# Tiles that TensorE reads in a hybrid decoder layer, placed at multiples of 128 bytes

## Chip, cores and metric

The kernel runs on one core of one Trainium2 chip. The time is the device time of one launch in microseconds, the median of several runs. The profile is one execution of the same program, with every engine's instructions.

## The reference, cut to what matters

One decoder layer over 256 tokens of width 2048, batch 1, float32: a mixer of sliding-window attention beside a Mamba-2 state space part, then a causal convolution FFN.

```python
def _hybrid_mixer(xn, w_in, ...):
    proj = xn @ w_in                       # 2048 -> 9248 columns: q, k, v, z, xbc, dt
    ...
    attn = _rmsnorm(_sliding_window_attention(q, k, v, sinks), attn_out_norm)
    xbc = jax.nn.silu(_causal_dwconv(xbc, ssd_conv_w, ssd_conv_b))
    ...
    y = _ssd_chunked(xs, dt, a, bm, cm) + ssd_d[:, None] * xs
    y = _gated_group_rmsnorm(y, z, ssd_norm)
    return jnp.concatenate([attn, y], axis=-1) @ w_out      # 4096 -> 2048

def _conv_ffn(hn, w_up, ffn_conv_w, ffn_conv_b, w_down):
    u = _causal_dwconv(hn @ w_up, ffn_conv_w, ffn_conv_b)   # 2048 -> 11264
    gate, val = u[..., :D_FF], u[..., D_FF:]
    return (jax.nn.silu(gate) * val) @ w_down               # 5632 -> 2048

h = x
h = h + _hybrid_mixer(_rmsnorm(h, norm_mix), ...)
h = h + _conv_ffn(_rmsnorm(h, norm_ffn), ...)
return _rmsnorm(h, norm_final)
```

The weights are 2048 x 9248, 4096 x 2048, 2048 x 11264 and 5632 x 2048 numbers, float32. Each is read once.

## The kernel before

All large products run in the type float32r, which TensorE takes at one column a cycle. To keep float32 accuracy each operand is split in two parts, hi and lo, with hi + lo equal to the number, and a product is three matmuls: hi x hi, hi x lo and lo x hi.

The weights come in blocks of 1 MB through SyncE's queue into raw (three buffers of 8704 bytes a partition). `split` makes hi on ScalarE (L70) and lo on VectorE (L72; a fourth of them on GpSimd while the mixers run) into four buffers each, 4352 bytes a partition. The activations lie transposed, channels on partitions, with both parts side by side: xT (the normed input), later h2T in the same place, attT (attention's output) and yT (the state space part's output), each 128 partitions x 16 channel tiles x 2 parts x 256 tokens.

The large products come in two forms. `gemm_tok` holds the activations stationary and moves 512 columns of weights (L156 to L158): keys with dt first (cut into 256 and 288 columns), values, four of queries and four of z from xT, then eight of the output projection from attT and yT. The down projection (`w_down_part`, `down`) has the same three lines with gs, the two parts of the gated activations of one channel tile, as the stationary operand. `gemm_chan` holds the weights stationary and moves activations: in the state space part three matmuls of 256 columns (L217 to L219, `wide=False`); in the up projection one of 512 columns, both parts of h2T at once under hi (L225), and one of 256 columns under lo (L223).

In a row such as `L156 PE MATMUL acc<-hi,xT` the first name behind the arrow is the moving operand, the second the stationary one.

The order is: keys and values (to about 80 us), four query products with attention beside them (to about 280 us), the state space part with three products a turn (to about 525 us), output projection (to 705 us), up projection with its convolutions (to 1190 us), down projection and the final norm. Work beside the large products is put between their turns by `later` and `step`; a scheduler of the tile framework then sets each engine's order. Tiles are placed by pools: a pool lays its tiles one behind the other in the order in which they are first asked for, each at a multiple of 32 bytes unless the tile asks for another multiple.

`steps_dt` works out the time steps of the state space part (softplus by a series) on VectorE, with four tiles sp0 to sp3 of 256 bytes a partition; `rope`, which rotates keys and queries, has two tiles rpa and rpb of 512 bytes.

Of the kernel before, what the change touches and what calls it, by code (L numbers as in the profile page):

```python
# [10 lines left out]
F32 = mybir.dt.float32  # L11
F32R = mybir.dt.float32r
# [35 lines left out]
def hymba(ctx, tc, x, xt, w_kd, w_in, w_out, w_up, w_down, par, vecs, gfin, con, out):  # L48
# [16 lines left out]
    share = [0, 0]  # L65

    def split(raw, o, n):
        hi = wp.tile([P, RAWW // 2], F32R, tag="hi", name="hi", bufs=4)
        lo = wp.tile([P, RAWW // 2], F32R, tag="lo", name="lo", bufs=4)
        A.copy(out=hi[:, :n], in_=raw[:, o : o + n])  # L70
        share[1] += 1
        (G if share[0] and share[1] % share[0] == 0 else V).tensor_tensor(  # L72
            out=lo[:, :n], in0=raw[:, o : o + n], in1=hi[:, :n].bitcast(F32), op=ALU.subtract
        )
        return hi, lo

    def pieces(src, width, parts, load=None, work=None):
        """the parts of a block's splits; load, work: what goes before a part's load and split."""
        raw = wp.tile([P, RAWW], F32, tag="raw", name="raw", bufs=3)
# [14 lines left out]
    xT = cp.tile([P, NKT, 2, S], F32R, tag="xT", name="xT")  # L94
# [22 lines left out]
    def rstd(dst, ss, n):  # L117
        """dst = (ss / n + EPS) ** -0.5, a column for each of the token tiles."""
# [4 lines left out]
    def rows_of(dst, r):  # L123
        """dst[p, t] = r of token t, on every partition."""
# [7 lines left out]
    def split_T(dst, kt, src, g, view=lambda a: a):  # L132
        """dst[:, kt] = the two parts of src * g."""
# [6 lines left out]
    def transpose_split(src, ct0, dst, kt0, n, gbase):  # L140
        """src [tokens, t, channels] to the parts of its transpose, n channel tiles times their weights."""
# [18 lines left out]
    # work beside the large products: steps that come up so many turns after they are called for  # L160
# [13 lines left out]
    def gemm_tok(blocks, actT, evac, width=2048, cuts=((0, 512),), tag="acc", parts_of=None):  # L174
        """out[token, column]: activations stationary, weights moving."""
# [24 lines left out]
    def gemm_chan(blocks, actT, evac, tag="acc", wide=True):  # L200
        """out[channel, token]: weights stationary, activations moving; wide: in two sums for evac to add."""
# [29 lines left out]
    def conv(dst, b, rB, wcol, bias, taps, wide):  # L231
        """dst = causal convolution over tokens of b * rB, channels on partitions."""
        u = up.tile([P, S], F32, tag="cu", name="cu", bufs=3)
# [14 lines left out]
    attT = mixctx.enter_context(tc.tile_pool(name="mp0", bufs=1)).tile([P, NKT, 2, S], F32R, name="attT")  # L248

    # =========== attention ===========  # L250
# [10 lines left out]
    def norm_x():  # L261
# [3 lines left out]
        for h in range(2):  # L265
            xq = wp.tile([P, RAWW], F32, tag="raw", name="x_r", bufs=3)[:, :D].rearrange("p (t d) -> p t d", t=NT)
# [11 lines left out]
    def rope(tl, t, nh):  # L278
        """rotate the first ROT dims of each head of tl[:, t] (nh heads), in place."""
# [26 lines left out]
    x_of = lambda kt: (xT, kt)  # noqa: E731  # L306
# [33 lines left out]
    # time steps: dt = softplus(dtx), cumulated dt * a  # L340
    nd = NT * NH
    f2 = lambda a: a.rearrange("p t h -> p (t h)")  # noqa: E731
# [6 lines left out]
    def steps_dt():  # L349
        ta, tb, tcc, td = (ap.tile([P, nd], F32, tag=f"sp{i}", name=f"sp{i}") for i in range(4))  # L350
# [50 lines left out]
    share[0] = 4  # part of the splits on GpSimd, beside what VectorE does for the mixers  # L401
# [5 lines left out]
    # values of two heads in two parts, with zeros on both sides: [v | 0] and [0 | v]  # L407
# [6 lines left out]
    def attention(c, q_t):  # L414
        """steps for two key-value heads 2 * c + jj and their query heads, q_t [P, t, (g, jj), HD]."""
        # on the partitions the two parts of a query beside each other, and for each of them the key's
# [34 lines left out]
        def scores(jj):  # L451
# [4 lines left out]
            for n in range(NT):  # L456
# [3 lines left out]
                for g0 in range(0, QPK, nh):  # L460
# [14 lines left out]
                    if n:  # L475
                        # the window: of each key's place in its block, either block's or none of it
# [27 lines left out]
        def probs_T(jj):  # L504
            """probabilities in two parts, keys on partitions; of the second block those of either block's keys."""
# [64 lines left out]
    # =========== state space ===========  # L570
# [419 lines left out]
```

## Time and profile before

| | us |
|---|---|
| median of 3 runs | 1442.59 |
| lowest and highest | 1442.48, 1445.29 |
| span of the profiled execution | 1442.0 |
| TensorE busy in it, 7925 matmuls | 1406.4 |
| VectorE busy | 989.6 |
| ScalarE busy | 772.0 |
| GpSimd busy | 269.4 |

The busy time of TensorE counts from a matmul's start to its modelled end, and consecutive matmuls overlap; how fast it goes is read from the distance between starts. PE in the rows is TensorE's matmuls, PEld its weight loads, DVE VectorE, ACT ScalarE, POOL GpSimd. The profile was taken on the one core that the kernel uses.

### The profile page before, as it was taken

How to read it: one execution, taken by the hardware profiler on the slowest of the kernel's cores; microseconds unless marked ns; L12 is line 12 of the kernel's file. 1: busy time of each engine (PE TensorE's matmuls, PEld its weight loads, DVE VectorE, ACT ScalarE, POOL GpSimd, SP SyncE). 2: the span in 40 equal slices, each digit the busy share in tenths (PEclk: the TensorE clock that was granted, in tenths of full speed). 3: DMA queues.
4: the chain of work that ended last, by engine and by line, in shares of the span. 5: the costliest groups of instructions: out<-in, count | busy, mean ns of one | idle time of the engine just before them, and what ended most of it. 6: DMA issues, size and time to landing. Idle time of an engine off the chain costs nothing.

```text
span 1442.0 us, 20476 instructions
## 1 busy us (share of the span) xinstructions
PE 1406.4 (98%) x7925; PEld 1231.3 (85%) x7925; DVE 989.6 (69%) x1454; ACT 772.0 (54%) x1209; POOL 269.4 (19%) x187
## 2 busy tenths in 40 slices
PE   8999999899999999999999999999999999999997
PEld 8888888789999988888888888888888888888886
DVE  6579999788685755555577776867767767545555
ACT  6565677456555554344465554555555554444444
POOL 0124544443434330000000111101111001000001
PEclk9999999999999999999999999999999999999999
DMA  8643333445545456554655555555555455555552
GB/s 317 237 166 125 117 118 117 140 153 190 182 172 186 155 175 257 179 201 175 226 180 195 187 181 200 187 193 190 190 187 192 176 204 190 190 204 182 197 199 94
DMA packets 40561, 263.37 MB, mean 183 GB/s; under 512 B 4608, under 2 KB 5248, under 8 KB 10640
## 3 DMA queue, kind: packets, MB, share of 16 engines
q1 hardware_dynamic: 38560, 254.69, 49.4%
q0 software_dynamic: 1904, 7.37, 1.8%
q8 instruction: 62, 1.02, 0.3%
q14 instruction: 35, 0.29, 0.1%
HBM read 259.92 MB, written 2.13 MB: 182 GB/s over the span
## 4 chain that ended last, share of the span: by engine, by line
PE 81%; DVE 10%; ACT 3%; issue 3%; POOL 1%; DMA 1%; SPq 0%; DVEq 0%; POOLq 0%; ACTq 0%
PE acc L225 11%; PE aux L225 11%; PE acc L158 10%; PE acc L157 10%; PE acc L156 10%; PE aux L223 6%; PE acc L223 6%; PE aux L156 3%; PE aux L157 3%; PE aux L158 3%; DVE lo L72 3%; DVE u L242 2%; PE acc L219 1%; PE acc L218 1%; PE acc L217 1%
## 5 line engine op out<-in xcount | busy, mean ns | idle before, releaser
L72 DVE TENSOR_TENSOR lo<-raw,hi 128x1024 fp32r<-128x1024 f32 (+2 forms) x442 | 550.0, 1250 | 348.9 <-ACT hi L70 348.3
L70 ACT CAST hi<-raw 128x1024 fp32r<-128x1024 f32 (+2 forms) x474 | 492.2, 1047 | 451.7 <-PE acc L158 135.3
L225 PE MATMUL acc<-h2T,hi 128*128 128x512 f32 x704 | 243.4, 391 | 0.0
L225 PE MATMUL aux<-h2T,hi 128*128 128x512 f32 x704 | 243.0, 391 | 0.0
L223 PE MATMUL aux<-h2T,lo 128*128 128x256 f32 x704 | 191.1, 282 | 0.0
L223 PE MATMUL acc<-h2T,lo 128*128 128x256 f32 x704 | 191.0, 282 | 0.0
L225 PEld LDWEIGHTS aux<-h2T,hi 128*128 128x128 f32 x704 | 129.8, 188 | 24.6
L225 PEld LDWEIGHTS acc<-h2T,hi 128*128 128x128 f32 x704 | 129.8, 188 | 24.5
L217 PE MATMUL acc<-xT,hi 128*128 128x256 f32 x512 | 145.4, 285 | 0.0
L218 PE MATMUL acc<-xT,hi 128*128 128x256 f32 x512 | 144.7, 283 | 0.0
L219 PE MATMUL acc<-xT,lo 128*128 128x256 f32 x512 | 143.9, 282 | 0.0
L817 POOL TENSOR_TENSOR gT<-gate,cv 128x256 f32<-128x256 f32 x44 | 61.2, 1392 | 434.5 <-DVE cv L242 424.0
L223 PEld LDWEIGHTS acc<-h2T,lo 128*128 128x128 f32 x704 | 132.9, 189 | 3.9
L223 PEld LDWEIGHTS aux<-h2T,lo 128*128 128x128 f32 x704 | 132.9, 189 | 3.8
L156 PE MATMUL acc<-hi,xT 128*128 128x512 f32 (+1 forms) x320 | 117.6, 387 | 6.4 <-ACT hi L70 5.7
L157 PE MATMUL acc<-lo,xT 128*128 128x512 f32 (+1 forms) x320 | 122.5, 386 | 0.6 <-DVE lo L72 0.6
L158 PE MATMUL acc<-hi,xT 128*128 128x512 f32 (+1 forms) x320 | 122.1, 384 | 0.0
L72 POOL TENSOR_TENSOR lo<-raw,hi 128x1024 fp32r<-128x1024 f32 x32 | 82.7, 2584 | 146.3 <-ACT hi L70 146.2
L218 PEld LDWEIGHTS acc<-xT,hi 128*128 128x128 f32 x512 | 97.1, 190 | 0.4
L217 PEld LDWEIGHTS acc<-xT,hi 128*128 128x128 f32 x512 | 97.0, 190 | 0.4
L219 PEld LDWEIGHTS acc<-xT,lo 128*128 128x128 f32 x512 | 96.9, 190 | 0.2
L156 PEld LDWEIGHTS acc<-hi,xT 128*128 128x128 f32 x320 | 60.4, 195 | 17.1 <-ACT hi L70 5.7
(224 smaller groups left out, 2421.9 us busy)
## 6 DMA issues: line engine op xcount, KB each, us to landing
raw<-in_w_up SPq DMA_DIRECT2D x88, 1024.0 KB, 4.8
raw<-in_w_in SPq DMA_DIRECT2D x68, 1024.0 KB, 4.8
raw<-in_w_down SPq DMA_DIRECT2D x44, 1024.0 KB, 4.8
raw<-in_w_out SPq DMA_DIRECT2D x32, 1024.0 KB, 4.8
e<-acs_d POOLq DMA_DIRECT2D x8, 512.0 KB, 6.2
raw<-in_w_kd SPq DMA_DIRECT2D x6, 544.0 KB, 7.8
x_r<-in_x SPq DMA_DIRECT2D x2, 1024.0 KB, 5.3
h<-in_x POOLq DMA_DIRECT2D x4, 512.0 KB, 7.5
```

The lines of the kernel that those rows point to most:

```text
L70: A.copy(out=hi[:, :n], in_=raw[:, o : o + n])
L72: (G if share[0] and share[1] % share[0] == 0 else V).tensor_tensor(out=lo[:, :n], in0=raw[:, o : o + n], in1=hi[:, :n].bitcast(F32), op=A ...
L156: PE.matmul(out=o, lhsT=lh, rhs=rh, start=first, stop=False)
L157: PE.matmul(out=o, lhsT=lh, rhs=rl, start=False, stop=False)
L158: PE.matmul(out=o, lhsT=ll, rhs=rh, start=False, stop=last)
L217: PE.matmul(out=b[ct][:, :S], lhsT=wh, rhs=rh, start=kt == 0, stop=False)
L218: PE.matmul(out=b[ct][:, :S], lhsT=wh, rhs=actT[:, kt, 1, :], start=False, stop=False)
L219: PE.matmul(out=b[ct][:, :S], lhsT=wl, rhs=rh, start=False, stop=end)
L223: PE.matmul(out=b[ct][:, :S], lhsT=wl, rhs=rh, start=False, stop=False)
L225: PE.matmul(out=b[ct], lhsT=wh, rhs=actT[:, kt, :, :], start=kt == 0, stop=end)
L242: V.scalar_tensor_tensor(out=dst[:, j:], in0=u[:, : S - j], scalar=wcol(taps - 1 - j), in1=dst[:, j:], op0=ALU.mult, op1=ALU.add,)
L817: G.tensor_tensor(out=gT[:, i, :], in0=gate[:, ct, :], in1=dst, op=ALU.mult)
```

## The change

Tiles that TensorE reads in the large products, and some that stand between them in a pool, are asked for with `align_bytes=128`: hi, lo, raw (and x_r in its place), xT, h2T, attT, yT, gs, gT, and the convolutions' u, gate and cu. So that the space suffices, two of the four tiles of `steps_dt` are no longer their own but rpa and rpb. Comments and docstrings are gone too.

```diff
 def split(raw, o, n):
-    hi = wp.tile([P, RAWW // 2], F32R, tag="hi", name="hi", bufs=4)
-    lo = wp.tile([P, RAWW // 2], F32R, tag="lo", name="lo", bufs=4)
+    hi = wp.tile([P, RAWW // 2], F32R, tag="hi", name="hi", align_bytes=128, bufs=4)
+    lo = wp.tile([P, RAWW // 2], F32R, tag="lo", name="lo", align_bytes=128, bufs=4)
...
-    raw = wp.tile([P, RAWW], F32, tag="raw", name="raw", bufs=3)
+    raw = wp.tile([P, RAWW], F32, tag="raw", name="raw", align_bytes=128, bufs=3)
...
-xT = cp.tile([P, NKT, 2, S], F32R, tag="xT", name="xT")
+xT = cp.tile([P, NKT, 2, S], F32R, tag="xT", name="xT", align_bytes=128)
...
-    u = up.tile([P, S], F32, tag="cu", name="cu", bufs=3)
+    u = up.tile([P, S], F32, tag="cu", name="cu", align_bytes=128, bufs=3)
...
-attT = mixctx.enter_context(tc.tile_pool(name="mp0", bufs=1)).tile([P, NKT, 2, S], F32R, name="attT")
+attT = mixctx.enter_context(tc.tile_pool(name="mp0", bufs=1)).tile([P, NKT, 2, S], F32R, name="attT", align_bytes=128)
...
 def steps_dt():
-    ta, tb, tcc, td = (ap.tile([P, nd], F32, tag=f"sp{i}", name=f"sp{i}") for i in range(4))
+    ta, tb, tcc, td = (ap.tile([P, nd], F32, tag=t, name=t, bufs=1) for t in ("sp0", "sp1", "rpa", "rpb"))
...
-    gs = fp.tile([P, 2, S], F32R, tag="gs", name="gs", bufs=4)
+    gs = fp.tile([P, 2, S], F32R, tag="gs", name="gs", align_bytes=128, bufs=4)
```

yT, h2T, gT, gate, x_r and the state space u change in the same way. Where the tiles stand in the two built programs, as the address of a partition's first byte modulo 128 and modulo 256 (all buffers of a name agree, and the slices that the large products read begin at multiples of 256 bytes within a tile, those of the key product at multiples of 128):

| tile | before, mod 128 | before, mod 256 | after, mod 128 | after, mod 256 |
|---|---|---|---|---|
| xT, h2T | 0 | 128 | 0 | 128 |
| hi, lo | 96 | 96 | 0 | 128 |
| attT, yT, gs | 96 | 96 | 0 | 0 |
| con_t (identity, masks) | 0 | 128 | 96 | 224 |
| qs, ks (query and key parts) | 32 | 160 | 64 | 64 |
| vs (value parts) | 32 | 160 | 64 | 64 |
| pt, po (probability parts) | 96 | 96 | 0 | 0 |

The order of instructions is the same on TensorE, ScalarE, GpSimd and SyncE. On VectorE it differs in one place, at about 47 us, where the time steps (L351 to L368) run between the rotations of the keys (L286 to L295) and the splits (L72); sp and rpa, rpb are the tiles named above:

```order
 L351 SCALAR_TENSOR_TENSOR sp_492<-dtx 128x64
-L364 TENSOR_SCALAR sp_495<-dtx 128x64
 L286 TENSOR_TENSOR rpa<-k_t,con_t 128x128
 L287 TENSOR_TENSOR rpb<-k_t,con_t 128x8x8
```

```order
 L355 TENSOR_SCALAR sp_493<-sp_492 128x64
+L364 TENSOR_SCALAR rpb<-dtx 128x64
 L356 RECIPROCAL sp_493<-sp_493 128x64
 L357 TENSOR_TENSOR sp_492<-sp_492,sp_493 128x64
 L358 TENSOR_TENSOR sp_493<-sp_492 128x64
-L359 TENSOR_SCALAR sp_494<-sp_493 128x64
-L360 TENSOR_TENSOR sp_494<-sp_494,sp_493 128x64
```

The maximum of dtx with zero (L364) stands before the second rotation's first rows in the kernel before and behind the first step of the series now; the rest of the series keeps its place under other names.

## Rows read from the trace of the kernel before

**Rows 1.** The page: span, and granted clock in 40 slices (9 is full).

```profile
span 1442.0 us, 20476 instructions
...
PEclk9999999999999999999999999999999999999999
```

**Rows 2.** The chain, shares by line, of 80-280, 340-525, 525-705, 705-1190, 1190-1430 us.

```profile
by line: issue 10.6%; DVE lo L72 9.9%; DVE u L242 8.4%; DVE pt L524 7.0%; PE acc L158 5.8%; PE acc L156 5.8%; PE acc L157 5.6%; ACT sm L486 4.4%; ACT hi L70 4.0%; DVE rs L496 3.7%; POOL sm L499 3.3%; DVE pt L515 3.1%; DVE sm L479 2.9%; DVE 
...
by line: PE acc L157 11.9%; PE acc L156 11.9%; PE acc L158 11.9%; DVE lo L72 8.9%; DVE u L242 6.8%; PE acc L219 6.3%; PE acc L218 6.2%; PE acc L217 6.1%; issue 6.0%; PE aux L653 4.7%; ACT hi L70 3.2%; DMA e<-acs_d 2.7%; POOL rg L121 2.5%; P
...
by line: PE acc L158 32.4%; PE acc L157 32.3%; PE acc L156 32.3%; PE aux L147 1.9%; PE acc L225 0.9%; PE acc L223 0.3%
...
by line: PE acc L225 32.7%; PE aux L225 32.6%; PE acc L223 17.3%; PE aux L223 17.2%; PE aux L147 0.2%; PE aux L129 0.1%
...
by line: PE acc L156 16.6%; PE acc L158 16.6%; PE acc L157 16.6%; PE aux L156 15.9%; PE aux L158 15.9%; PE aux L157 15.8%; PE aux L225 1.0%; DVE h L865 0.6%; ACT jk L867 0.6%; PE aux L223 0.5%; issue 0.1%; DVE s L894 0.0%; ACTq L867 0.0%
```

**Rows 3.** Tiles xT, yT, gs: matmuls, duration ns least/median/most, first and last start.

```profile
L157 PE MATMUL acc<-lo,xT x17: 395/395/396, 98.3 to 109.5; 128*128 128x512 f32 x17
...
L156 PE MATMUL acc<-hi,yT x32: 389/389/389, 547.7 to 568.8; 128*128 128x512 f32 x32
...
L157 PE MATMUL acc<-lo,gs x90: 389/389/389, 1239.6 to 1360.0; 128*128 128x512 f32 x90
```

**Rows 4.** The same of xT at 385-402.5 us and of h2T at 840-1000 us.

```profile
L218 PE MATMUL acc<-xT,hi x51: 277/280/282, 384.8 to 402.3; 128*128 128x256 f32 x51
...
L225 PE MATMUL acc<-h2T,hi x250: 390/390/397, 839.6 to 992.9; 128*128 128x512 f32 x125
...
L223 PE MATMUL aux<-h2T,lo x212: 277/282/282, 860.0 to 999.9; 128*128 128x256 f32 x106
```

**Rows 5.** Timeline of TensorE in attention's values: start us, duration, instruction.

```profile
164.90 0.28 PE L156 MATMUL aux<-pt,vs 128*128 128x256 f32 x1
...
165.69 0.28 PE L157 MATMUL aux<-po,vs 128*128 128x256 f32 x1
165.81 0.28 PE L158 MATMUL aux<-po,vs 128*128 128x256 f32 x1
```

**Rows 6.** Groups of TensorE over the span: matmuls, busy us, mean ns.

```profile
L225 PE MATMUL acc<-h2T,hi 128*128 128x512 f32 x704 | 243.4, 391 | 0.0
...
L217 PE MATMUL acc<-xT,hi 128*128 128x256 f32 x512 | 145.4, 285 | 0.0
...
L156 PE MATMUL acc<-hi,xT 128*128 128x512 f32 x256 | 102.5, 405 | 0.7 <-DVE rs L497 0.7
...
L156 PE MATMUL acc<-hi,gs 128*128 128x512 f32 x176 | 67.7, 389 | 0.0
...
L156 PE MATMUL acc<-hi,yT 128*128 128x512 f32 x128 | 49.8, 389 | 0.0
```

**Rows 7.** Timeline of TensorE where transposes break into attT's products.

```profile
534.29 0.39 PE L158 MATMUL acc<-hi,attT 128*128 128x512 f32 x1
534.52 0.60 PE L147 MATMUL aux<-con_t,y 128*128 128x128 f32 x4
...
535.19 0.40 PE L157 MATMUL acc<-lo,attT 128*128 128x512 f32 x1
...
535.66 0.40 PE L156 MATMUL acc<-hi,attT 128*128 128x512 f32 x1
```

**Rows 8.** Weight loads: xT at 98.5-109.9 us, yT at 548-569 us.

```profile
L156 PEld LDWEIGHTS acc<-hi,xT 128*128 128x128 f32 x17 | 3.2, 188 | 0.8
...
L156 PEld LDWEIGHTS acc<-hi,yT 128*128 128x128 f32 x31 | 5.8, 188 | 1.2
```

**Rows 9.** Busy us of PE, PEld, DVE, ACT, POOL at 800-840; then tile dtx.

```profile
800.00:840.00 40.00, 40.00 (x233) 35.35 (x232) 28.49 (x43) 22.37 (x34) 4.66 (x4) 1.00 0.55 202
...
L375 PEld LDWEIGHTS aux<-dtx,con_t x2: 188/188/189, 62.5 to 62.7; 128*128 128x128 f32 x2
...
L364 DVE TENSOR_SCALAR sp<-dtx x1: 186/186/186, 47.6 to 47.6; 128x64 f32<-128x64 f32 x1
```

More of the change, by code (lines that the diff above doesn't have):

```diff
@@ L265, in norm_x @@
         for h in range(2):
-            xq = wp.tile([P, RAWW], F32, tag="raw", name="x_r", bufs=3)[:, :D].rearrange("p (t d) -> p t d", t=NT)
+            xq = wp.tile([P, RAWW], F32, tag="raw", name="x_r", align_bytes=128, bufs=3)[:, :D].rearrange("p (t d) -> p t d", t=NT)
             SY.dma_start(out=xq, in_=xrows[:, :, h * 1024 : (h + 1) * 1024])
@@ L688, in open_sp @@
         apctx.close()
-        yT = mixctx.enter_context(tc.tile_pool(name="mp1", bufs=1)).tile([P, NKT, 2, S], F32R, name="yT")
+        yT = mixctx.enter_context(tc.tile_pool(name="mp1", bufs=1)).tile([P, NKT, 2, S], F32R, name="yT", align_bytes=128)
         sp = spctx.enter_context(tc.tile_pool(name="sp", bufs=1))
@@ L710, in hymba @@
         for g in (2 * zi, 2 * zi + 1):
-            u = up.tile([P, 4, S], F32, tag="u", name="u", bufs=2)
+            u = up.tile([P, 4, S], F32, tag="u", name="u", align_bytes=128, bufs=2)
             def evac_u(ct, b, u=u, g=g):
@@ L755, in hymba @@
     hp = h2 = None
-    h2T = cp.tile([P, NKT, 2, S], F32R, tag="xT", name="h2T")
+    h2T = cp.tile([P, NKT, 2, S], F32R, tag="xT", name="h2T", align_bytes=128)
     ss2 = cp.tile([P, NT, 4], F32, name="ss2")
@@ L801, in hymba @@
     fp = ctx.enter_context(tc.tile_pool(name="fp", bufs=1))
-    gT = fp.tile([P, NFT, S], F32, name="gT")
+    gT = fp.tile([P, NFT, S], F32, name="gT", align_bytes=128)
     gf = fp.tile([P, D], F32, name="gf")
@@ L805, in hymba @@
     for c in range(11):
-        gate = up.tile([P, 4, S], F32, tag="u", name="gate", bufs=2)
+        gate = up.tile([P, 4, S], F32, tag="u", name="gate", align_bytes=128, bufs=2)
         def evac_f(ct, b, val, c=c, gate=gate):
```

## The prediction

> **What bounds the kernel now.** I read the page first: a span of 1442.0 us with the granted clock full in every slice [rows 1], so that TensorE runs at its 2.4 GHz level and 512 columns stream in 512 / 2.4 = 213.3 ns, 256 columns in 106.7 ns. Then the chain of waits, stretch by stretch [rows 2]. From 525 us to 1430 us it is TensorE's matmuls almost alone: 97% of the output projection, 99.8% of the up projection (L223 and L225), 97% of the down projection (L156 to L158). In these 905 us a nanosecond saved on each matmul is saved on the span. Between 80 and 340 us and up to 525 us the mixers take turns with VectorE, GpSimd and DMA: matmuls with xT as the stationary tile hold only 5.8 + 5.8 + 5.6 = 17.2% of the chain in 80-280 us and 35.7% in 340-525 us. In 340-525 us the three 256-column lines (L217 to L219) hold another 18.6%.
>
> The number that matters is the distance from one matmul's start to the next one's, not its listed duration. I take it from first and last starts of undisturbed stretches. Stationary yT, moving hi or lo: the 31 steps from 547.7 to 568.8 us are 93 matmuls, 21.1 / 93 = 226.9 ns. Stationary gs: 531 matmuls lie between the first and the last start of that row, 120.4 / 531 = 226.7 ns. Stationary xT, the same code and the same moving tiles: 16 steps of three from 98.3 to 109.5 us, 11.2 / 48 = 233.3 ns [rows 3]. With the parts changed over, weights stationary and xT moving 256 columns: 17.5 / 150 = 116.7 ns. In the up projection the four groups hold 250 + 250 + 212 + 212 = 924 matmuls between 839.6 and 999.9 us: 160.3 / 923 = 173.7 ns, so 347.3 ns for a pair of one 512-column and one 256-column matmul [rows 4]. The small value products of attention, 256 columns, stand 0.79 / 7 = 113 ns apart from 164.90 to 165.69 us, with one more 0.12 us behind them [rows 5]. So every matmul pays a surplus over its streaming time, 6 to 20 ns, and it differs between places that run the same shape.
>
> **What the surplus goes with.** Taking these places by the table of addresses: yT and gs, at 96 modulo 128, under moving tiles at 96: surplus 13.5 ns. xT at 0 under moving tiles at 96: 20.0 ns. Weights at 96 under xT at 0: 10.0 ns. Values at 32 under probabilities at 96: 6.3 ns. An unaligned address alone does not cost more (the cheapest place has two, and xT, the one aligned stationary tile, is the dearest); what the rows are compatible with is that the distance between the two addresses that TensorE reads at once counts. The change makes that distance zero modulo 128 in all large products. Of same shape and distance zero there are yT, attT and gs, so their 226.8 ns is my price for a 512-column matmul after the change. A weight load by itself lasts 188 ns from xT and from yT alike [rows 8], so the load alone gains nothing.
>
> **The change part by part.**
> 1. Stationary xT (query, z and value products). L156 to L158 have 256 each with xT in acc [rows 6], 768, and the value product 96 more by its loops, 864 in all. Each goes from 233.3 to 226.8 ns: 864 x 6.5 = 5.6 us. Of that the chain holds 17.2% of 200 us = 34.4 us and 35.7% of 185 us = 66 us; 6.5 / 233.3 of these 100 us is 2.8 us, and the value product, which runs ahead of the mixers with TensorE on the path, gives 96 x 6.5 = 0.6 us. So 3.4 us on the path, 5.6 us if the other engines follow. I take 4 us off.
> 2. Up projection, 1408 pairs (704 of L225 in acc and as many in aux) [rows 6]. Today 347.3 ns. The 512-column matmul at 226.8 ns and the 256-column one at what chan shows, 116.7 ns, make 343.5 ns: 3.8 ns off a pair, 5.4 us. If the 256-column one also takes the full 13.5 ns of yT, 120.2 ns, the pair is 347.0 ns and the gain 0.4 us. At the 113 ns of the values, 339.8 ns and 10.6 us. Nearest in kind are the first two; the middle, 2.9 us off.
> 3. The 256-column products of the state space part, 3 x 512 = 1536 matmuls [rows 6]. Distance zero could bring 113 ns (5.7 us off) or 120.2 ns (5.4 us on); on the chain stands a third of them at most. Ends -2 and +2 us; I take 0.
> 4. attT, yT and gs, 6 x 128 + 6 x 176 = 1824 matmuls [rows 6]. Distance zero before and after: 0. Ends: with the 6.3 ns surplus of the values each would save 7.2 ns, 13.1 us; with xT's 20.0 ns it would lose 6.5 ns, 11.9 us.
> 5. Small products. The identity and the masks move from 0 to 96, the query, key and value tiles from 32 to 64. Some 300 transposes and small matmuls by a few ns each way: under 1 us, 0 taken.
> 6. The time steps. Two tiles of the softplus chain become rpa and rpb, and L364 (0.19 us at 47.6 us [rows 9]) moves behind the rotation of the keys. All of it is VectorE work, in order on one engine; nothing of another engine waits in between but the first reader, TensorE's L375, whose weights load only at 62.5 us [rows 9]. Cover: some microseconds; without it 0.2 us. Taken as 0.
> 7. No transfer, tile count or queue changes, and all else keeps its order. A faster TensorE asks the splits to come sooner: at 800-840 us VectorE is busy 28.5 and ScalarE 22.4 of 40 us [rows 9], so a pace 1% higher meets no new bound there.
>
> Sum: -4 - 2.9 = -6.9 us on 1442.0 us of span; the profiled span and the median of the runs are 0.6 us apart, so 1442.6 - 6.9 = 1435.7, rounded to 1436 us.
>
> **The rivals.**
> *Addresses don't matter (or the change, in effect, does nothing).* For it: in attT's stretch, with unchanged addresses, the matmuls behind a block of transposes stand 0.47 / 2 = 235 ns apart for a while and last 0.40 instead of 0.39 us [rows 7]. So 233 ns can also be a state of TensorE's pipeline that xT's stages happen to stay in. And xT and h2T, half of the operands in question, stand at a multiple of 128 already. Against it: the clean value of yT and gs never settles in xT's stages. Time: 1442.6 us. The Trainium skill, TensorE: Matmul & The Clock Gate, section Part 2: What happens when you issue a matmul, states that TensorE has two independent read ports and that loading the next weights takes no bandwidth from the running matmul. By that rule the distance of two addresses could cost nothing and this rival would hold; the three different surpluses of one shape speak against it without settling it.
> *Alignment itself counts.* No large product today has both operands aligned. If the surplus then falls to the smallest that a row shows, 6.3 ns, the 1824 matmuls of part 4 save 7.2 ns each (13.1 us, 97% on the path: 12.7), the up projection 347.3 - 219.6 - 113 = 14.7 ns a pair (20.7 us), xT's 13.7 ns of 233.3 on 100 us of chain plus the value product (5.9 + 1.3 us), part 3 some 2 us: about 42 us, 1400 us. The same skill page, section Back-to-back issue gap, gives the columns over 2.4 GHz plus 2.5 ns, 215.8 ns for 512 columns; an estimate by it would take another 3.8 ns from each 512-column matmul. No row here shows that value. Against this rival: the cheapest place today is unaligned on both sides.
> *Slower: the period is 256 bytes, not 128.* Multiples of 128 that differ by 128 are then a distance. After the change hi, lo and xT stand at 128 modulo 256, attT, yT and gs at 0; before, all but xT stood at 96. The output and down projections, 1824 matmuls, would go from 226.8 towards xT's 233.3 ns: 11.9 us, 97% on the path, 11.5 us on; xT's stages and the up projection still gain 6.9 us. Net +4.6: 1447 us. It decides as soon as the loss is over 3.7 ns a matmul.
>
> **How the numbers follow.** Forecast 0.42, no effect 0.27, alignment itself 0.18, slower 0.13. What a measurement of this kernel tells from no change is about 0.2%, 2.9 us. The forecast's own range is 1431 to 1441 us (part 2's and part 1's ends); some 0.06 of it lies within 0.2%. So faster 0.36 + 0.18 = 0.54, same 0.27 + 0.06 = 0.33, slower 0.13. The range runs from 1405 us, which leaves out the better half of the second rival (0.09), to 1448 us, which leaves out the outer part of the slower one (0.06).
>
> **What would show it.** Right: the distance of starts in xT's stages falls to 227 ns, the up projection's pair falls to 343 to 347 ns, yT and gs stay at 227 ns. xT still at 233 ns: addresses don't matter. yT and gs at 220 ns or less: alignment itself. yT and gs over 230 ns: the period is longer than 128 bytes. What would make the prediction wrong is a price at both-aligned that none of today's places shows.

## The result, and the profile after

The changed kernel takes 1462.36 us (1461.57 to 1463.13), the kernel before 1442.53 us (1442.39 to 1445.29) beside it. The ratio is 1.0136, with a 95% interval of 1.0122 to 1.0151: slower by 1.4%, some 20 us. The forecast was 1436 us and the range ended at 1448 us, so the sign and the range were both wrong.

The page of the changed kernel. The span is 17.5 us longer [rows 1], the count of instructions and the granted clock are the same: no work was added and the clock stayed at its 2.4 GHz level.

```profile
span 1459.5 us, 20476 instructions
...
PEclk9999999999999999999999999999999999999999
```

In the runs after, the time lies 2.1 us above the span of the same execution (1461.57 over 1459.5). By that, the profiled execution of before took about 1444.1 us, 1.6 us above its median, while the profiled one after lies 0.8 us below its own; so the spans differ by 17.5 us and the medians by 19.8 us.

Where the time came from is told by the stages' first starts. TensorE's rows by stationary or moving tile, of the kernel before (count; ns shortest/median/longest; first and last start; shape):

```profile
L156 PE MATMUL acc<-hi,attT x128: 387/389/477, 525.0 to 680.4; 128*128 128x512 f32 x128
...
L225 PE MATMUL acc<-h2T,hi x704: 390/390/481, 702.8 to 1170.7; 128*128 128x512 f32 x176
...
L156 PE MATMUL acc<-hi,gs x176: 389/389/392, 1193.2 to 1426.4; 128*128 128x512 f32 x176
...
L156 PE MATMUL aux<-hi,gs x176: 389/389/389, 1195.9 to 1431.9; 128*128 128x512 f32 x176
```

The same rows of the changed kernel:

```profile
L156 PE MATMUL acc<-hi,attT x128: 390/393/482, 523.0 to 682.1; 128*128 128x512 f32 x128
...
L225 PE MATMUL acc<-h2T,hi x704: 390/398/481, 705.1 to 1180.9; 128*128 128x512 f32 x176
...
L156 PE MATMUL acc<-hi,gs x176: 387/396/398, 1203.8 to 1443.8; 128*128 128x512 f32 x176
...
L156 PE MATMUL aux<-hi,gs x176: 392/398/398, 1206.5 to 1449.4; 128*128 128x512 f32 x176
```

| stage (from first start to the next stage's) | before, us | after, us | difference |
|---|---|---|---|
| mixers, to attT's first | 525.0 | 523.0 | -2.0 |
| output projection | 177.8 | 182.1 | +4.3 |
| up projection | 490.4 | 498.7 | +8.3 |
| down projection, to the last start of L156 in aux | 238.7 | 245.6 | +6.9 |
| rest | 10.1 | 10.1 | 0 |
| span | 1442.0 | 1459.5 | +17.5 |

The loss is in the three stages where the chain of waits was TensorE's matmuls almost alone [rows 2]; the mixers, where waits take turns, even gained. The listed durations hardly say it (a median of 389 ns becomes 393 to 398); the distance between starts does. The rows of the changed kernel that answer to [rows 3] and [rows 4], each in about the same stretch: first tile xT stationary.

```profile
L156 PE MATMUL acc<-hi,xT x17: 389/389/401, 96.5 to 107.4; 128*128 128x512 f32 x17
```

Tile yT stationary, and the first and last row of gs (six such rows of 86):

```profile
L158 PE MATMUL acc<-hi,yT x31: 392/398/399, 546.7 to 567.7; 128*128 128x512 f32 x31
...
L157 PE MATMUL aux<-lo,gs x86: 391/396/399, 1239.7 to 1359.4; 128*128 128x512 f32 x86
...
L156 PE MATMUL aux<-hi,gs x86: 392/396/398, 1241.5 to 1359.8; 128*128 128x512 f32 x86
```

xT moving 256 columns in the state space part, and h2T in the up projection:

```profile
L218 PE MATMUL acc<-xT,hi x51: 282/283/284, 383.3 to 401.3; 128*128 128x256 f32 x51
...
L225 PE MATMUL acc<-h2T,hi x256: 395/398/404, 841.9 to 1000.0; 128*128 128x512 f32 x128
L223 PE MATMUL acc<-h2T,lo x256: 277/281/284, 842.2 to 999.9; 128*128 128x256 f32 x128
L225 PE MATMUL aux<-h2T,hi x198: 395/398/404, 839.8 to 977.4; 128*128 128x512 f32 x198
L223 PE MATMUL aux<-h2T,lo x198: 277/281/285, 840.1 to 977.3; 128*128 128x256 f32 x198
```

The working is that of the prediction: 10.9 / 48 for xT, 21.0 / 90 for yT, 120.1 / 515 for gs, 18.0 / 150 for the 256 columns, 160.2 / 907 x 2 for the pair. Beside each stands what the table of addresses makes of it: the **distance**, which from here on is the moving tile's address minus the stationary tile's, modulo 256 bytes.

| product | distance before | ns before | distance after | ns after |
|---|---|---|---|---|
| xT stationary, 512 columns | 224 | 233.3 | 0 | 227.1 |
| yT, gs stationary, 512 columns | 0 | 226.9, 226.7 | 128 | 233.3, 233.2 |
| weights stationary, xT moving 256 columns | 32 | 116.7 | 0 | 120.0 |
| up projection, pair of 512 and 256 columns | 32 | 347.3 | 0 | 353.2 |

The first two lines change places. All tiles of these products stand at multiples of 128 now, but hi, lo and xT at 128 and attT, yT, gs at 0 modulo 256, so the pair that had been equal is half a period apart. The last two lines got distance zero and became dearer.

### The profile page after: what moved, and what is told of

It reads as the page before. It is cut to its first block, busy times and chain, and to the rows that moved or that the text cites. A ratio compares the mean times of both kernels' runs of the same rounds, so it can differ in the third digit from the quotient of the medians.

```text
span 1459.5 us, 20476 instructions
## 1 busy us (share of the span) xinstructions
PE 1425.3 (98%) x7925; PEld 1234.2 (85%) x7925; DVE 989.7 (68%) x1454; ACT 771.2 (53%) x1209; POOL 270.0 (18%) x187
## 4 chain that ended last, share of the span: by engine, by line
PE 85%; DVE 8%; ACT 2%; issue 2%; DMA 1%; POOL 1%; SPq 0%; DVEq 0%; POOLq 0%; ACTq 0%
PE aux L225 11%; PE acc L225 11%; PE acc L158 10%; PE acc L157 10%; PE acc L156 10%; PE acc L223 6%; PE aux L223 6%; PE aux L157 3%; PE aux L156 3%; PE aux L158 3%; PE acc L218 3%; PE acc L219 3%; PE acc L217 3%; DVE lo L72 2%; DVE u L242 2%
## 5 line engine op out<-in xcount | busy, mean ns | idle before, releaser
L72 DVE TENSOR_TENSOR lo<-raw,hi 128x1024 fp32r<-128x1024 f32 (+2 forms) x442 | 549.9, 1249 | 363.6 <-ACT hi L70 362.4
L225 PE MATMUL acc<-h2T,hi 128*128 128x512 f32 x704 | 247.3, 399 | 0.0
L225 PE MATMUL aux<-h2T,hi 128*128 128x512 f32 x704 | 247.1, 399 | 0.0
L217 PE MATMUL acc<-xT,hi 128*128 128x256 f32 x512 | 147.1, 288 | 0.0
L218 PE MATMUL acc<-xT,hi 128*128 128x256 f32 x512 | 146.5, 287 | 0.0
L156 PE MATMUL acc<-hi,xT 128*128 128x512 f32 (+1 forms) x320 | 116.1, 382 | 6.6 <-ACT hi L70 6.1
L158 PE MATMUL acc<-hi,xT 128*128 128x512 f32 (+1 forms) x320 | 120.2, 378 | 0.0
L72 POOL TENSOR_TENSOR lo<-raw,hi 128x1024 fp32r<-128x1024 f32 x32 | 82.1, 2564 | 144.3 <-ACT hi L70 134.7
L218 PEld LDWEIGHTS acc<-xT,hi 128*128 128x128 f32 x512 | 98.9, 193 | 0.3
L217 PEld LDWEIGHTS acc<-xT,hi 128*128 128x128 f32 x512 | 98.7, 193 | 0.4
L156 PEld LDWEIGHTS acc<-hi,xT 128*128 128x128 f32 x320 | 60.0, 194 | 16.4 <-ACT hi L70 6.3
```

The source lines that it names most:

```text
L156: PE.matmul(out=o, lhsT=lh, rhs=rh, start=first, stop=False)
L158: PE.matmul(out=o, lhsT=ll, rhs=rh, start=False, stop=last)
L217: PE.matmul(out=b[ct][:, :S], lhsT=wh, rhs=rh, start=kt == 0, stop=False)
L218: PE.matmul(out=b[ct][:, :S], lhsT=wh, rhs=actT[:, kt, 1, :], start=False, stop=False)
L225: PE.matmul(out=b[ct], lhsT=wh, rhs=actT[:, kt, :, :], start=kt == 0, stop=end)
```

## The experiments

The theory after the result: a 512-column matmul is cheap when the distance modulo 256 is zero, and each shape and order has its own cheapest distance. Its rivals: the address of each tile by itself counts; or what other engines read and write at the same time, which the addresses also change. But for the time steps, all variants of the whole kernel below have the same instructions in the same order, engine by engine, as the kernel they start from, by their traces; only hi and lo begin some elements of 4 bytes further on within their tiles, by a number `shift[0]` that is set before a product:

```diff
-    share = [0, 0]
+    share, shift = [0, 0], [0]
...
-        hi = wp.tile([P, RAWW // 2], F32R, tag="hi", name="hi", align_bytes=128, bufs=4)
+        hi = wp.tile([P, RAWW // 2], F32R, tag="hi", name="hi", align_bytes=128, bufs=4)[:, shift[0] : shift[0] + n]
```

and lo likewise. Each is compared with the kernel before, run on the same chip.

**TensorE alone, distance swept.** A small kernel that does nothing but repeat one matmul, with a stationary tile sa at 0 or sd at 96 and eight moving tiles wa to wh at 0, 32, ... 224 modulo 256, and three more at 4, 8 and 16 (PHASES is the letters a to h, n is 48):

```diff
+    sa = at("sa", 0, xr, 512)
+    sd = at("sd", 24, xr, 512)
...
+    ws = {c: at("w" + c, 8 * i, raw, 512) for i, c in enumerate(PHASES)}
...
+        for i in range(n):
+            PE.matmul(out=b, lhsT=s[:, i % 4 * P : (i % 4 + 1) * P], rhs=m, start=i == 0, stop=i == n - 1)
```

> This kernel leaves the whole layer out: it loads two blocks and runs TensorE alone, 48 matmuls of 512 columns a group under one stationary tile (72 of 256 columns, or 36 pairs of 512 and 256), where only the address of one operand changes by 32 bytes from group to group. sa stands at 0 modulo 256, sd at 96, wa to wh at 0, 32, ... 224, wi, wj, wk at 4, 8 and 16. Theory A (the distance of the moving operand from the stationary one, modulo 256, sets the surplus): under sa, 512 columns at 227 ns for wa (distance 0), 233 ns for we (128) and for wh (224); under sd the same values three names later, so wd (96) gives 227 and wa no longer does. With weights stationary and sa moving 256 columns: wa 120 ns, wh (distance 32) 117 ns, wc (distance 192) 113 ns. Pairs: wa 354 ns, wh 347 ns. Rival B (a start at a multiple of 128 is dear or cheap in itself): the values of sd follow the names as those of sa do, wa and we alike. Rival C (concurrent work of the other engines makes the difference): all groups of one form within 1 ns of each other.

TensorE's rows for tile sd:

```profile
L56 PE MATMUL acc<-wa,sd x48: 392/397/402, 158.8 to 169.9; 128*128 128x512 f32 x48
L56 PE MATMUL acc<-wb,sd x48: 388/393/398, 170.1 to 181.0; 128*128 128x512 f32 x48
L56 PE MATMUL acc<-wc,sd x48: 389/395/398, 181.3 to 192.2; 128*128 128x512 f32 x48
L56 PE MATMUL acc<-wd,sd x48: 389/389/395, 192.5 to 203.1; 128*128 128x512 f32 x48
L56 PE MATMUL acc<-we,sd x48: 393/396/399, 203.4 to 214.3; 128*128 128x512 f32 x48
L56 PE MATMUL acc<-wf,sd x48: 388/392/398, 214.6 to 225.3; 128*128 128x512 f32 x48
L56 PE MATMUL acc<-wg,sd x48: 392/394/402, 225.6 to 236.5; 128*128 128x512 f32 x48
L56 PE MATMUL acc<-wh,sd x48: 392/395/398, 236.8 to 247.7; 128*128 128x512 f32 x48
```

From one group's first start to the next one's are 48 matmuls: 11.3, 11.2, 11.2, 10.9, 11.2, 11.0, 11.2 us, that is 233 to 235 ns but for wd with 227 and wf with 229. Tile wd is the one that stands at 96 like sd (distance 0), wf the one at distance 64. Under sa, at 0, the single starts give 226.7 ns for wa, 228.9 for wc (64) and 233 to 234 for the others, the one at 128 among them. So two tiles at 96 are as fast as two at 0: the address by itself doesn't count, and no other engine is needed for the effect. The order of the up projection was tried in the same kernel, and there I was wrong: with weights wa stationary, at distance zero, the pair took 12.1 / 35 = 346 ns, where the theory expected 354 ns, the changed kernel having shown 353.2.

```profile
L73 PE MATMUL acc<-sa,wa x36: 391/391/398, 316.2 to 328.3; 128*128 128x512 f32 x36
```

The 256-column matmuls in it, weights stationary, lay between 117.3 and 120.0 ns at all eight distances, with 0 and 96 the dearest. The 113 ns of the attention's value products [rows 5], expected at distance 192, did not come back: 117.8 ns. Two stationary tiles in turn, one of them at distance 0, gave 230 and 232 ns, which does not tell whether the weights of the running matmul or those of the next one are what counts.

**Output and down projection at distance zero again.** The changed kernel with hi and lo 128 bytes on in these two:

```diff
-    hp = h2 = None
+    hp = h2 = None; shift[0] = 32
...
-    G.dma_start(out=gf, in_=gfin.partition_broadcast(P))
+    G.dma_start(out=gf, in_=gfin.partition_broadcast(P)); shift[0] = 0
...
-    oacc = [[acc("acc" if t == 0 else "aux") for _ in range(4)] for t in range(NT)]
+    oacc = [[acc("acc" if t == 0 else "aux") for _ in range(4)] for t in range(NT)]; shift[0] = 32
```

> The changed kernel with hi and lo read and written 128 bytes further on in the output and the down projection, so that they stand at 0 modulo 256 like attT, yT and gs; all instructions and their order as in the changed kernel. Theory A: L156 to L158 with attT, yT and gs fall from 232 to 237 ns back to 227 ns, 1824 matmuls by about 5.5 ns: 10 us off, about 1452 us; xT's products and the up projection as in the changed kernel. Rival B (the multiple of 128 itself): both operands stay at multiples of 128, so nothing moves, 1462 us.

It takes 1449.49 us, ratio 1.0044 (1.0029 to 1.0059). TensorE's rows for attT, h2T and gs:

```profile
L156 PE MATMUL acc<-hi,attT x128: 389/389/476, 521.1 to 676.4; 128*128 128x512 f32 x128
...
L225 PE MATMUL acc<-h2T,hi x704: 391/398/478, 698.9 to 1174.6; 128*128 128x512 f32 x176
...
L156 PE MATMUL acc<-hi,gs x176: 388/389/389, 1197.4 to 1430.7; 128*128 128x512 f32 x176
...
L156 PE MATMUL aux<-hi,gs x176: 389/389/389, 1200.1 to 1436.1; 128*128 128x512 f32 x176
```

The output projection is 698.9 - 521.1 = 177.8 us long and the down projection 1436.1 - 1197.4 = 238.7 us, to the tenth as before; the up projection stays at 498.5 us. Both stages together give back 11.2 us. The medians differ by 12.9 us; most of the rest lies in the mixers, which ended 1.9 us earlier though nothing in them differs from the changed kernel: by so much, about 2 us, one profile differs from another there.

**The up projection at its old distance.** The changed kernel with hi and lo 224 bytes on there alone (distance 32):

```diff
-    G.dma_start(out=gf, in_=gfin.partition_broadcast(P))
+    G.dma_start(out=gf, in_=gfin.partition_broadcast(P)); shift[0] = 56
...
-    oacc = [[acc("acc" if t == 0 else "aux") for _ in range(4)] for t in range(NT)]
+    oacc = [[acc("acc" if t == 0 else "aux") for _ in range(4)] for t in range(NT)]; shift[0] = 0
```

> The changed kernel with hi and lo 224 bytes further on in the up projection alone, so that they stand 32 bytes behind h2T as before the change (96 under 128 modulo 256). Theory A: the pair of L225 and L223 goes from 354 back to 347 ns, 1408 pairs by 7 ns: 9 to 10 us off, about 1453 us; output and down projection stay at 232 to 237 ns. Rival B: here the weights leave the multiple of 128, so a gain would also fit B; what tells them apart is that the first experiment gains as well. Rival D (the up projection is slower because its convolutions' tiles gate, cu and gT were moved): nothing changes, 1462 us.

It takes 1452.97 us, ratio 1.0063 (1.0046 to 1.0080). TensorE's rows for h2T and gs:

```profile
L225 PE MATMUL acc<-h2T,hi x704: 390/390/482, 705.6 to 1173.5; 128*128 128x512 f32 x176
...
L156 PE MATMUL acc<-hi,gs x176: 390/393/404, 1196.0 to 1435.1; 128*128 128x512 f32 x176
```

1196.0 - 705.6 = 490.4 us, as before. The up projection's 8.3 us come from the distance of its two operands alone.

**Both undone.** The changed kernel with shifts of 32, 56 and 32 elements in the output, up and down projection:

```diff
-    hp = h2 = None
+    hp = h2 = None; shift[0] = 32
...
-    G.dma_start(out=gf, in_=gfin.partition_broadcast(P))
+    G.dma_start(out=gf, in_=gfin.partition_broadcast(P)); shift[0] = 56
...
-    oacc = [[acc("acc" if t == 0 else "aux") for _ in range(4)] for t in range(NT)]
+    oacc = [[acc("acc" if t == 0 else "aux") for _ in range(4)] for t in range(NT)]; shift[0] = 32
```

> The changed kernel with hi and lo 128 bytes further on in the output and down projections and 224 bytes further on in the up projection: distances as before the change there, 0 in xT's products (before: 224) and 0 in the 256-column products of the state space part (before: 32). Theory A: the two gains add, 1462.4 - 12.9 - 9.4 = 1440 us; against the kernel before it gains xT's 3 to 5 us and loses the state space part's share of 3 ns on 1536 matmuls, 0 to 4 us: 1438 to 1443 us. A rival by which the two places hide each other: over 1446 us.

1442.26 us, ratio 0.9988 (0.9978 to 0.9998); the three stages stand at 177.8, 490.4 and 238.7 us, and the span is 1440.1 us, 19.4 us under that of the changed kernel. The two stages' 11.2 us of the first variant and the 8.3 us of the second make 19.5. All else that the change does, the other tiles' places and the time steps among it, costs nothing that shows.

**The time steps by themselves.** The kernel before with that one line of the change:

```diff
-    ta, tb, tcc, td = (ap.tile([P, nd], F32, tag=f"sp{i}", name=f"sp{i}") for i in range(4))
+    ta, tb, tcc, td = (ap.tile([P, nd], F32, tag=t, name=t, bufs=1) for t in ("sp0", "sp1", "rpa", "rpb"))
```

> The kernel before with only the four tiles of the time steps changed (two of them rpa and rpb), no tile of the large products moved. Theory A: 1442.5 us, within 0.1%. Rival E (the shared tiles of the time steps hold up VectorE or TensorE): up to 20 us more.

1443.39 us, ratio 0.9999 (0.9989 to 1.0008). The shared tiles and the moved L364 cost nothing that shows, at most 0.1%.

**xT alone at distance zero.** The kernel before, with hi and lo 32 bytes on in the value, query (which follow the value product with the same shift) and z products, where xT is stationary:

```diff
-    gemm_tok([w_in[0, i] for i in range(4)], x_of, evac_v, tag="aux", parts_of=parts_v)
+    shift[0] = 8; gemm_tok([w_in[0, i] for i in range(4)], x_of, evac_v, tag="aux", parts_of=parts_v)
...
-            gemm_chan([w_in[5 + 3 * zi + g % 2, i] for i in range(4)], xT, evac_u, wide=False)
+            shift[0] = 0; gemm_chan([w_in[5 + 3 * zi + g % 2, i] for i in range(4)], xT, evac_u, wide=False)
...
-        gemm_tok([w_in[7 + 3 * zi, i] for i in range(4)], x_of, evac_z)
+        shift[0] = 8; gemm_tok([w_in[7 + 3 * zi, i] for i in range(4)], x_of, evac_z)
...
-    hp = h2 = None
+    hp = h2 = None; shift[0] = 0
```

> The kernel before, all tiles at their old places, with hi and lo 32 bytes further on in the value, query and z products alone, so that xT's 864 matmuls go from distance 224 to distance 0. Theory A: 233 to 227 ns there, 3.4 us off by the share that these matmuls have in the chain, at most 5.6 us: 1437 to 1440 us against 1443, and nothing else moves. If TensorE's gain were eaten by VectorE in the mixers: within 1 us of the kernel before.

1441.27 us against 1443.48 us of the kernel before on that chip, ratio 0.9979 (0.9971 to 0.9987). This is the lowest ratio of all kernels here, though the intervals of two others below 1 overlap with it, and it holds the one gain that the prediction had right: 3.0 us by the ratio (1.9 to 4.2), 2.2 us by the medians. TensorE's row for attT begins at 522.4 us, 2.6 us earlier than in the kernel before:

```profile
L156 PE MATMUL acc<-hi,attT x128: 389/389/476, 522.4 to 677.8; 128*128 128x512 f32 x128
```

**The distance swept inside the whole kernel.** The changed kernel with another shift in each product, and in the down projection another one after every five or six channel tiles:

```diff
-        gemm_tok([w_in[1 + c, i] for i in range(4)], x_of, evac_q)
+        shift[0] = 8 * (2 * c + 1); gemm_tok([w_in[1 + c, i] for i in range(4)], x_of, evac_q)
...
-            gemm_chan(
+            shift[0] = 8 * ((2 * c + val) % 8); gemm_chan(
...
     def w_down_part(kt):
-        gs = fp.tile([P, 2, S], F32R, tag="gs", name="gs", align_bytes=128, bufs=4)
+        shift[0] = kt * 8 // NFT * 8; gs = fp.tile([P, 2, S], F32R, tag="gs", name="gs", align_bytes=128, bufs=4)
```

> The changed kernel with hi and lo shifted by another 32 bytes from product to product, so that every form runs at all eight distances in place (down projection: one distance for 5 or 6 channel tiles; up projection: one for each of eight products in turn; state space: one for each group). Theory A: the down projection at 227 ns for distance 0, 229 for 64, 233 to 234 for the other six, as with TensorE alone; 256 columns: 120 ns at 0 and 96, 117 to 118 at the rest; pairs near 347 ns at 32 and 160, over 350 ns elsewhere, and at 0 the 354 ns of the changed kernel although TensorE alone had 347 there. If a distance decided nothing by itself in the full kernel, the products' pitches would not follow the distance.

Matmuls with gs in seven stretches of 28.00 us, at distances 128, 160, 192, 224, 0, 32 and 64 in this order; columns: stretch, its length, busy time of TensorE and count in it, granted clock, DMA share, GB/s:

```profile
1203.00:1231.00 28.00, 28.00 (x122) 1.00 0.53 188
1234.00:1262.00 28.00, 28.00 (x121) 1.00 0.53 187
1264.00:1292.00 28.00, 28.00 (x122) 1.00 0.55 188
1295.70:1323.70 28.00, 28.00 (x121) 1.00 0.53 188
1326.00:1354.00 28.00, 28.00 (x125) 1.00 0.56 188
1356.40:1384.40 28.00, 28.00 (x122) 1.00 0.56 191
1386.00:1414.00 28.00, 28.00 (x124) 1.00 0.55 188
```

The count includes matmuls cut by the stretch's ends. Distance 0 takes in 125, distance 64 takes in 124, all others 121 or 122: the same two cheap distances as with TensorE alone, 226.7 and 228.9 ns by the single starts, the others 233.3 to 234.3 (96, not shown, among them). The clock is full and DMA busy at nearly the same share throughout (0.53 to 0.56). The up projection's pair stood at 347.5 ns at distance 32, 347.4 at 160, 350.5 at 96, 351.0 at 128, 353.0 at 64, 192 and 224, and 353.2 at 0 (in two of three products; the first comes back below). So in this kernel the old distance 32 was one of the two best for the up projection, and zero among the worst. In the state space part, with one group for each distance, 64 and 192 looked cheapest, at 115 and 116 ns against 117 to 120.

**xT at zero and the state space part at 64.** The variant with xT alone at zero, with one number changed:

```diff
-            shift[0] = 0; gemm_chan([w_in[5 + 3 * zi + g % 2, i] for i in range(4)], xT, evac_u, wide=False)
+            shift[0] = 56; gemm_chan([w_in[5 + 3 * zi + g % 2, i] for i in range(4)], xT, evac_u, wide=False)
```

> The kernel before with hi and lo at the distances that were cheapest in the sweep in place: 0 in the value, query and z products (before: 224), 64 in the 256-column products of the state space part (before: 32), 32 in the up projection and 0 in output and down projection as before. Theory A: the 2.2 us of the run with xT's products alone, and up to 2 ns on the 1536 matmuls of 256 columns, a third of them on the chain, another 1 us: ratio 0.997 to 0.998 to the kernel before. If the cheaper distance 64 was an accident of two groups in the sweep: the same as with xT's products alone, 0.998.

1441.98 us, ratio 0.9984 (0.9975 to 0.9993): no better than with xT alone. Over the whole state space part the pitch (the distance from start to start) was 118 ns, against 117 ns at the old distance 32, and not the 115 ns of the sweep's one group, so that reading was an accident of the group.

**The state space part at its old distance.** The changed kernel with a shift of 56 elements there alone (distance 32):

```diff
-            gemm_chan([w_in[5 + 3 * zi + g % 2, i] for i in range(4)], xT, evac_u, wide=False)
+            shift[0] = 56; gemm_chan([w_in[5 + 3 * zi + g % 2, i] for i in range(4)], xT, evac_u, wide=False)
```

> The changed kernel with hi and lo 224 bytes further on in the 256-column products of the state space part alone, so that their distance is 32 again as before the change. Theory A: 120 ns falls to 117 to 118 ns on 1536 matmuls; a third of these lie on the chain: 1 to 2 us off, about 1461 us. If they count in full: 4 us off. Up, output and down projections stay as slow as in the changed kernel.

1459.22 us, ratio 1.0099 (1.0084 to 1.0115). By the medians that is 3.1 us under the changed kernel; by the ratios, since the kernel before beside it stood 2.2 us higher here, it is some 5 us (2 to 8 by the two intervals, which just miss each other). TensorE's row for L217 in about the stretch of [rows 4]:

```profile
L217 PE MATMUL acc<-xT,hi x51: 277/280/282, 381.0 to 398.5; 128*128 128x256 f32 x51
```

17.5 / 150 = 116.7 ns, as before the change; the matmuls themselves give back 1536 x 3.3 ns = 5.1 us, of which a part is off the chain. So that undoing gains is shown, but not how much: in its profile the mixers ended at 520.6 us, 2.4 us before those of the changed kernel, yet only 0.5 us before those of the first variant, whose mixers are the changed kernel's.

**What the surplus is made of.** TensorE alone again; the matmul of 512 columns with fewer stationary columns, then with fewer moving ones, at distances 0, 32, 64 and 128; and the up projection's order (four accumulators in turn, two channel tiles, hi and lo) at distances 0, 32, 128 and 160:

```diff
+        for cols in (128, 64, 32):
+            for c in "abce":
+                tok(sa, ws[c], cols, 512)
+        for n in (448, 384, 320):
+            for c in "abce":
+                tok(sa, ws[c], P, n)
+        for c in "ahed":
+            up(hs[c], ls[c])
```

> This kernel leaves the layer out: TensorE alone, stationary sa at 0, moving wa, wb, wc, we at 0, 32, 64, 128 modulo 256. First 128, 64 and 32 stationary columns under 512 moving ones, then 128 stationary columns under 448, 384 and 320 moving ones, then the up projection's order of matmuls (two weight tiles, four sums) with the weights at 0, 224, 128 and 96 under activations at 0 (distances 0, 32, 128, 160). If the surplus comes from the weight load's reads meeting the moving operand's reads: with 64 and 32 stationary columns it shrinks, from 13 to 20 ns towards 3 to 10, and so does its dependence on the distance; and with fewer moving columns at 128 stationary ones it stays in nanoseconds. If it comes from the moving operand alone: unchanged with fewer stationary columns, and smaller in proportion with fewer moving ones. The up projection's order at distance 0: 354 ns a pair if the order of operands makes the difference to 347 ns in the first sweep, 347 ns if other engines do.

With 128 stationary columns the four distances gave 226.7, 233.4, 228.9 and 232.2 ns, with 64 columns 230.0, 230.8, 228.3 and 229.3, with 32 columns 231.7, 232.9, 231.7 and 230.7; a listed weight load lasts 188, 134 and 109 ns with them. A shorter weight load makes the distances alike, but not cheap: the surplus over 213.3 ns stays at 15 to 20 ns. If it were simply the time in which the next weights' reads get in the way of the moving columns, the surplus should have shrunk as its dependence on the distance did; in this simple form that reading falls. With 448 moving columns distance 0 was the dearest (206.7, 204.4, 200.0, 203.8), with 384 distance 128 (173.3, 173.3, 173.3, 176.0), with 320 all stood at 146.7. So which distance is cheap belongs to the shape. The least values of the four widths have something in common that none of these distances took away: 226.7, 200.0, 173.3 and 146.7 ns are each some 13.3 ns above their columns at 2.4 GHz (256 columns get down to 116.7 ns, 10.0 above). TensorE's rows with the up projection's order, L64 the 512-column matmuls at distances 0, 32, 128 and 160:

```profile
L64 PE MATMUL acc<-xu,ha x48: 392/398/403, 274.0 to 290.6; 128*128 128x512 f32 x48
...
L64 PE MATMUL acc<-xu,hh x48: 390/390/392, 291.0 to 307.3; 128*128 128x512 f32 x48
...
L64 PE MATMUL acc<-xu,he x48: 387/396/400, 307.6 to 324.1; 128*128 128x512 f32 x48
...
L64 PE MATMUL acc<-xu,hd x48: 391/392/397, 324.4 to 340.7; 128*128 128x512 f32 x48
```

Over 47 steps these are 353, 347, 351 and 347 ns: the values of the whole kernel, with no other engine at work.

**Why the pair at distance zero took 346 ns once.** The order of the up projection at distance zero, made simpler step by step towards the pair of the first small kernel: one channel tile instead of four (hb), one accumulator instead of four (hc), one weight tile instead of hi and lo (hd), all three (he):

```diff
+        up(hs["a"], ls["a"])
+        up(hs["b"], ls["b"], kts=1)
+        up(hs["c"], ls["c"], banks_n=1)
+        up(hs["d"], ls["d"], both=False)
+        up(hs["e"], ls["e"], banks_n=1, kts=1, both=False)
```

> This kernel leaves the layer out: TensorE alone, the up projection's pairs at distance 0 throughout. First its order in full (two weight tiles ha and la, four sums, four channel tiles of activations; 353 ns a pair in the sweep before), then with one channel tile (hb), with one sum (hc), with one weight tile for both matmuls of a pair (hd), and with all three simplifications (he), which is the pair that took 347 ns in the first sweep. Whichever simplification alone brings 347 ns is what the price at distance 0 hangs on; if none does but the last, it is their combination or the start of the stretch.

TensorE's rows for the fullest and the simplest:

```profile
L65 PE MATMUL acc<-xu,ha x48: 389/398/403, 41.4 to 58.0; 128*128 128x512 f32 x48
...
L65 PE MATMUL acc<-xu,he x48: 395/398/403, 109.2 to 125.8; 128*128 128x512 f32 x48
```

16.6 / 47 = 353 ns for both, and for the three between. None of the simplifications brings 346 ns back. One difference was left: he takes its weights from eight places, from the two halves of the tile by turns, where the first kernel's pair took four in a row. But the changed kernel's own trace has both values, at distance zero and within the first product of its up projection. TensorE's timeline (start us, duration, instruction):

```profile
714.97 0.40 PE L225 MATMUL acc<-h2T,hi 128*128 128x512 f32 x1
...
718.86 0.39 PE L225 MATMUL acc<-h2T,hi 128*128 128x512 f32 x1
719.09 0.38 PE L129 MATMUL aux<-diag,ones 128*128 128x128 f32 x2
...
719.43 0.39 PE L225 MATMUL acc<-h2T,hi 128*128 128x512 f32 x1
...
723.94 0.39 PE L225 MATMUL acc<-h2T,hi 128*128 128x512 f32 x1
```

Between the first two are 11 pairs, 3.89 / 11 = 354 ns; then two small matmuls with other tiles break in, and the 13 pairs behind them take 4.51 / 13 = 347 ns. Where the order of the two widths turns round at the end of the product, the pair goes back to 353 ns and stays there in the 21 products that follow. In the kernel before, at distance 32, it stands at 347 ns on both sides of the same break. So the same pair at the same distance can stand at two steady values, a break in the row of matmuls can take it from one to the other, and the 8.3 us are the price of staying at the dear one. Why a break leads to this one or that one stays open.

## Why the prediction was wrong

*Part 4 failed, and with it the sign.* The step "distance zero before and after: 0" took the distance modulo 128. It is zero modulo 256 that counts for 512 columns, and after the change these products are at 128: 226.8 to 233.2 ns, +11.2 us in the two stages. Rows 3 had xT at a distance of 96 modulo 128 and could not tell the periods apart; no row showed a distance of exactly 128. The table of addresses did show that the change makes one. The rival with a period of 256 named the mechanism and its price, +11.5 us, rightly, though with luck in the price: it took that of xT's distance, 224, for distance 128, and at 64 the sweep has 228.9 ns. It got 0.13 where nothing in the rows spoke for the shorter period. (Two slips that change nothing: that rival turns slower from 6.9 us / 1824 = 3.8 ns a matmul on, not 3.7; and the rows show two surpluses of each shape, not three of one.)

*Part 2 failed, with the sign too.* It added the price of a 512-column matmul at distance zero (226.8 ns, from yT) and that of a 256-column one (116.7 to 120.2 ns) to a pair of 343.5 to 347.0 ns. The pair measured 353.2 ns, +8.3 us. The price of one shape, taken where it follows itself, doesn't carry over to two shapes in turn: distance 32, dear for 512 columns alone, is among the two best for the pair, and at zero the pair has a second, dearer steady value that no row of before showed. The range of this term ended at no gain; a loss was excluded by no reason, and should have been in it. The slower rival carried the same fault, and so ended at 1447 us instead of near the 1462 us measured: its two stages were right, its 6.9 us of gain elsewhere were a loss of 6.3 us (8.3 lost, 2.0 gained).

*Part 3 was mis-sized.* Of the ends -2 and +2 the value 0 was taken. The pitch went to the upper price, 120.0 ns, and undoing it brought some 5 us by the ratios (2 to 8), 3.1 us by the medians.

*Part 1 was right:* 233.3 to 227.1 ns, and 3.0 us (1.9 to 4.2) where it stands alone, for the 4 us that were taken. It and part 3 pull against each other, and the mixers as a whole gained only about 2 us, which is also what one profile scatters by there: the four profiles with the changed kernel's mixers end them at 521.1 to 523.4 us, the two with those of before at 524.5 and 525.0.

*Nothing speaks against parts 5 to 7.* The time steps are at 0.9999, and with the three projections undone the kernel is back at 0.9988; the small products were not tried by themselves.

*The rival "alignment itself counts" fell* in the sweep: two tiles at 96 are as fast as two at 0. *That addresses don't matter* fell with every variant: 128 bytes of offset, with no instruction changed, are worth 11.2 us.

## What to carry to other kernels

For the two operands that TensorE reads at once in a float32r product, look at the difference of their addresses, not at each alignment, and ask whether the alignment that is asked for is as long as the period; a shorter one leaves the difference to the order of the pool, and here it made an equal pair unequal. Measure the price of a distance in the very shape and order in which the matmuls run, by start to start and not by their listed durations. An offset inside a tile, set for each product, is a cheaper tool than alignment: it changes one product and leaves all other tiles where they are.

## What the runs showed of the hardware

The distance modulo 256 bytes between moving and stationary operand is worth 2 to 8 ns of a 512-column float32r matmul: 226.7 ns at 0, 228.9 at 64, 232 to 234 at the other multiples of 32; 4 to 16 bytes off zero are no better (236.7, 233.3 and 231.7 at 4, 8 and 16). For the pair of 512 and 256 columns the order is another: 347 at 32 and 160, 350 to 351 at 96 and 128, 353 at 64, 192 and 224, and at 0 either 347 or 353. The Trainium skill, TensorE: Matmul & The Clock Gate, section Part 2: What happens when you issue a matmul, says that TensorE has two independent read ports and that the next weights are loaded without taking read bandwidth from the running matmul. Taken as a rule on time, the distance would be worth nothing by that; the measurements differ, and decide. Why the two operands' addresses act on each other is not shown by any run here.
